# Latent attention on one Trainium2 core: a branch's sum is copied out of PSUM by ScalarE and divided in place by VectorE

## The chip, the cores and the metric

One Trainium2 chip, one of its cores. The metric is device microseconds of one execution of the whole program, as the median of several runs. Lower is better. The program is written in a tile framework whose scheduler runs a timeline model of its own while it builds, and writes down each engine's instructions in the order that this model gives. Every engine then works through its own list strictly in order.

## The reference, cut to what matters

Two layers over 512 latent tokens with a context of 256 tokens. Layer 0 has attention, layer 1 recurrences; each ends in a PEER expert network (16 experts out of 16384 for each of 8 heads). The change lies in the latent attention of layer 0:

```
p = softmax(concat(scores of latent keys, scores of context keys, sink))
out = sum(p_i @ v_i)                       # 4 blocks of 128 queries
branch A: all 512 latent keys + 256 context keys, no sink
branch B: keys within 128 positions + 256 context keys, with sink
y = concat(A, B) @ w_out;   h = h + gate * y
```

Each branch has 8 heads of width 64. The kernel multiplies the values with unnormalised exponentials and divides by their sums afterwards.

## The kernel before

Layer 0 runs in these stages: modulation and context attention; the projections of context and latents; the latent attention (`attention`, L488, the loop at L531); then `peer_lat` (L916), the expert network of the latents. The context's own expert network is done by gathering: `gather_run` (L714) fetches, for each of two context blocks, 128 times 128 rows of `peer_u` and then 128 times 128 rows of `peer_v` by indirect DMA. One gather means one indirect DMA that GpSimd (POOL) issues (L722, L731) and one VectorE instruction over 128x1024 that uses it up: a product with a sum (L724), or a scaled addition to `gacc` (L736, the first at L734). Five buffers named `grow` hold gathered rows. L726 is the Gelu between the two halves, L739 and L740 close a block. These gathers have the lowest priority (L887), so the scheduler strews them over VectorE's list between everything else: they run during the latent attention and far into `peer_lat`. The latent block 0 (`REST`) is gathered likewise after them.

For each of 4 query blocks `att_block` (L432) does two branches. For each branch `attend` (L387) runs four times: TensorE makes scores into two `pbig` tiles (L401, L404, masks L407), VectorE takes the negated maximum (L411, with the sink L413), ScalarE the exponentials (L417), TensorE transposes them (L424), ScalarE copies them out of PSUM (L425), and TensorE multiplies with the values (L429) into one quarter of the bank `pv`, role "o", tile `po`. There is a single bank of that role (L530). After the fourth call VectorE inverts the sums (L453) and spreads them (L456), TensorE turns them (L459), ScalarE copies that out (L462), and VectorE multiplies `po` with it into half of `mT` (L463). Only then may the next branch's L429 write `po`. `out_block` (L236) multiplies `mT` with the output weights (L800), VectorE applies the gate (L221), GpSimd adds (L222), and `norm` (L533) makes the block's input of the expert network: L99 scales, L107 transposes, L115 shifts; for blocks 1 to 3 L123 and L124 split the result into two parts, `xh` and `xl`. `mT` has one buffer.

`peer_lat` can't start its products (L806, from `project`, L932) before the last block's `xl`. It then computes scores, picks experts, and runs 128 chunks of `hidden` (L817): load `u` (`peer_uT`), split it (L793 on ScalarE, L794 on VectorE), multiply (L806, L808). `peer_values` (L824) does the second half with `v` (L841, weighting L854), and L869 and L870 add its result to the latents. Layer 1 begins with L99 on the sums.

Of the kernel before, what the change touches and what calls it, by code (L numbers as in the profile page):

```python
# [18 lines left out]
AF = mybir.ActivationFunctionType  # L19
OP = mybir.AluOpType  # L20
# [30 lines left out]
class Kern:  # L51
# [380 lines left out]
    def att_block(self, pool, out, qT, b, lat):  # L432

        nc = self.nc
        if not lat:
            mix = pool.tile([128, D], F32, name="mix")
            for branch in range(2):
                for i in (0, 2):
                    for r in range(2):
                        self.attend_ctx(pool, qT, b, branch, r, i, mix)  # L440
            return self.mix_T(out, [mix[:, k * 128:(k + 1) * 128] for k in range(KD)])
        mT = out.tile([128, KD, 128], F32, name="mT", bufs=1)
        for branch in range(2):
            pv = self.pm("o")
            nm, sm = (pool.tile([128, 8], F32, name=x, bufs=2) for x in ("nm", "sm"))
            for i in range(4):
                self.attend(pool, qT, b, branch, i, pv, nm, sm)
            if branch:
                es = pool.tile([128, 8], F32, name="es", bufs=2)
                nc.vector.tensor_tensor(es, nm, self.sink, op=OP.add)  # L450
                nc.scalar.activation(es, es, AF.Exp)
                nc.vector.tensor_tensor(sm, sm, es, op=OP.add)
            nc.vector.reciprocal(sm, sm)  # L453

            x = pool.tile([128, 8, 64], F32, name="rcp")
            nc.vector.tensor_copy(x, sm.unsqueeze(2).to_broadcast([128, 8, 64]))  # L456
            pr = self.pm("a")
            for i in range(4):
                nc.tensor.matmul(pr[:, i * 128:(i + 1) * 128], x[:, 2 * i:2 * i + 2].rearrange("p h d -> p (h d)"),  # L459
                                 self.ident, start=True, stop=True)  # L460
            y = x.rearrange("p h d -> p (h d)")
            nc.scalar.activation(y, pr, AF.Copy)  # L462
            nc.vector.tensor_tensor(mT[:, 4 * branch:4 * branch + 4].rearrange("p c q -> p (c q)"), pv, y, op=OP.mult)  # L463
        return mT

    def att_out_ctx(self, pool, mTs):
# [1234 lines left out]
```

## Time and profile before

| | us |
|---|---|
| three runs | 4375.18, 4366.16, 4362.2; median 4366.16 |
| the profiled execution, its own time | 4357.14 |
| its span in the trace | 4355.4 |
| busy in the span: PE, DVE, ACT, POOL | 3926.1, 3415.4, 1783.2, 1520.6 |
| mean granted TensorE clock | 0.937 of full speed |

PE is TensorE's matmuls, PEld its weight loads, DVE VectorE, ACT ScalarE, POOL GpSimd. The page's shares are means over stages of different kinds, so the stages are read one by one: from a table of windows, then by what each engine waited for in a stage, then instruction by instruction in order of time. A row of the waits names the waiting instruction and what ended its wait; in the timeline the bracket behind a row holds the idle time before it and its releaser. Gathers have their DMA's cost apart from their VectorE cost: POOL only issues it.

### The profile page before, as it was taken

What the parts mean: (1) busy time and instruction counts of PE and PEld (TensorE: products, weight loads), DVE (VectorE), ACT (ScalarE), POOL (GpSimd) and SP (SyncE); (2) the same over time, 40 slices, a digit from 0 to 9 for tenths busy, and PEclk for the clock granted to TensorE, in tenths of its full rate; (3) what the DMA queues carried; (4) which work ended last, traced back from release to release, by engine and by line L of the source; (5) the groups of instructions that cost most, each with busy time, mean ns of one, the idle gap of its engine ahead of it and who ended that gap; (6) DMA issues with size and microseconds to landing.
All of it is one profiled execution on the core that took longest, in us unless ns stands there. A gap on an engine that the chain in (4) does not pass through costs nothing.

```text
span 4355.4 us, 63744 instructions
## 1 busy us (share of the span) xinstructions
PE 3926.1 (90%) x22484; PEld 3452.8 (79%) x22484; DVE 3415.4 (78%) x7022; ACT 1783.2 (41%) x3482; POOL 1520.6 (35%) x1252
## 2 busy tenths in 40 slices
PE   7995588799799888999999699999988999899998
PEld 5684356599789887778888569988988899888887
DVE  2249988899998898898899766665998888777555
ACT  3310243332345674434333433334234577433433
POOL 0016666655434445443444101221333333322000
PEclk9997588799999998999999799999999999999999
DMA  7748877899878999999999411022688999999765
GB/s 309 262 161 288 272 261 264 300 322 334 290 262 295 344 346 362 338 342 337 347 343 342 138 57 38 31 88 69 223 284 290 306 343 342 368 338 330 238 220 162
DMA packets 439674, 1152.81 MB, mean 265 GB/s; under 512 B 39173, under 2 KB 209541, under 8 KB 428089
## 3 DMA queue, kind: packets, MB, share of 16 engines
q1 hardware_dynamic: 289592, 586.63, 38.8%
q0 software_dynamic: 147456, 536.94, 35.2%
q10 hardware_dynamic: 2304, 25.17, 1.6%
q8 instruction: 177, 2.90, 0.3%
q14 instruction: 145, 1.18, 0.1%
HBM read 1045.30 MB, written 103.28 MB: 264 GB/s over the span
## 4 chain that ended last, share of the span: by engine, by line
PE 61%; DVE 16%; DMA 11%; issue 6%; ACT 4%; POOL 2%; SPq 0%; DVEq 0%; ACTq 0%; POOLq 0%
PE acc L841 23%; PE ph L806 8%; PE pa L806 6%; DMA u<-peer_uT 4%; DVE grow L724 4%; PE ph L808 3%; PE pa L808 3%; DMA grow<-peer_u,gidx 3%; PE pa L288 3%; DMA grow<-peer_v,gidx 2%; DVE gacc L736 2%; PE pt L780 2%; DVE ul L794 2%; PE pa L800 2%; PE pa L162 1%
## 5 line engine op out<-in xcount | busy, mean ns | idle before, releaser
L731 POOL DMA_INDIRECT grow<-peer_v,gidx x512 | 692.8, 1353 | 878.6 <-DVE gacc L736 739.7
L722 POOL DMA_INDIRECT grow<-peer_u,gidx x512 | 665.8, 1300 | 744.1 <-DVE hid L724 437.8
L806 PE MATMUL ph<-xh,uh 128*128 128x384 f32 x2048 | 722.9, 353 | 104.3 <-ACT uh L793 78.1
L806 PE MATMUL ph<-xl,uh 128*128 128x384 f32 x2048 | 710.0, 347 | 0.3 <-DVE xl L124 0.3
L736 DVE SCALAR_TENSOR_TENSOR gacc<-grow,gw,gacc 128x1024 f32<-128x1024 f32 x508 | 655.6, 1291 | 33.7 <-DMA grow<-peer_v,gidx 31.1
L724 DVE CUSTOM_DVE_ANT_0 grow<-grow,gx 128x1024 f32<-128x1024 f32 x512 | 620.8, 1224 | 48.1 <-DMA grow<-peer_u,gidx 45.1
L793 ACT ACTIVATE uh<-u 128x1024 fp32r<-128x1024 f32 x340 | 358.2, 1057 | 521.0 <-DMA u<-peer_uT 218.5
L794 DVE TENSOR_TENSOR ul<-u,uh 128x1024 fp32r<-128x1024 f32 x340 | 415.7, 1225 | 127.8 <-ACT uh L793 104.2
L806 PEld LDWEIGHTS ph<-xh,uh 128*128 128x128 f32 x2048 | 402.1, 196 | 128.1 <-ACT uh L793 93.2
L841 PE MATMUL acc<-vl,wh 128*128 128x512 f32 x1536 | 480.2, 394 | 1.6 <-DVE vl L794 1.6
L841 PE MATMUL acc<-vh,wl 128*128 128x512 f32 x1536 | 475.6, 391 | 0.0
L841 PE MATMUL acc<-vh,wh 128*128 128x512 f32 x1536 | 409.4, 396 | 17.4 <-ACT vh L793 9.9
L808 PE MATMUL ph<-xh,ul 128*128 128x384 f32 x2048 | 410.8, 339 | 7.0 <-DVE ul L794 6.7
L806 PEld LDWEIGHTS ph<-xl,uh 128*128 128x128 f32 x2048 | 402.7, 197 | 2.8 <-DVE xl L124 0.8
L793 ACT ACTIVATE wh<-w 128x384 fp32r<-128x384 f32 x256 | 134.3, 525 | 636.3 <-PE acc L841 496.4
L808 PEld LDWEIGHTS ph<-xh,ul 128*128 128x128 f32 x2048 | 359.8, 189 | 11.0 <-DVE ul L794 8.9
L794 DVE TENSOR_TENSOR vl<-v,vh 128x1024 fp32r<-128x1024 f32 x256 | 312.7, 1221 | 51.8 <-ACT vh L793 50.4
L841 PEld LDWEIGHTS acc<-vh,wh 128*128 128x128 f32 x1536 | 285.6, 189 | 75.1 <-ACT vh L793 11.8
L841 PEld LDWEIGHTS acc<-vh,wl 128*128 128x128 f32 x1536 | 288.7, 188 | 62.4 <-issue 0.9
L841 PEld LDWEIGHTS acc<-vl,wh 128*128 128x128 f32 x1536 | 286.2, 189 | 61.4 <-DVE vl L794 4.1
L793 ACT ACTIVATE vh<-v 128x1024 fp32r<-128x1024 f32 x256 | 270.0, 1056 | 48.6 <-PE acc L841 37.1
L780 PE MATMUL pt<-oi,oj 128*128 128x128 f32 x1536 | 211.5, 287 | 35.9 <-DVE oj L769 14.8
(549 smaller groups left out, 6570.4 us busy)
## 6 DMA issues: line engine op xcount, KB each, us to landing
u<-peer_uT SPq DMA_DIRECT2D x256, 512.0 KB
v<-peer_v SPq DMA_DIRECT2D x256, 512.0 KB
w<-mod_w SPq DMA_DIRECT2D x48, 1024.0 KB
Gd<-stage SPq DMA_DIRECT2D x48, 1024.0 KB
Hd<-hw SPq DMA_DIRECT2D x240, 192.0 KB
w<-Hd SPq DMA_DIRECT2D x240, 192.0 KB
u<-rec_w SPq DMA_DIRECT2D x52, 512.0 KB
g<-Gd SPq DMA_DIRECT2D x16, 1536.0 KB
```

What stands on the lines that cost most here:

```text
L288: nc.tensor.matmul(ps[:, b * 128:(b + 1) * 128], aT[:, kd, b * 128:(b + 1) * 128], w[:, kd, :], start=kd == 0, stop=kd == KD - 1)
L722: nc.gpsimd.indirect_dma_start(out=u, out_offset=None, in_=A[f"peer_u{layer}"], in_offset=bass.IndirectOffsetOnAxis(ap=row(s), axis=0))
L724: nc.vector.tensor_tensor_reduce(u, u, x, 1.0, 0.0, OP.mult, OP.add, hid[:, s:s + 1])
L731: nc.gpsimd.indirect_dma_start(out=u, out_offset=None, in_=A[f"peer_v{layer}"], in_offset=bass.IndirectOffsetOnAxis(ap=row(s), axis=0))
L736: nc.vector.scalar_tensor_tensor(acc, u, w[:, s:s + 1], acc, op0=OP.mult, op1=OP.add)
L780: nc.tensor.matmul(ps[:, t * 128:(t + 1) * 128], oj[:, t], oi[:, t], start=True, stop=True)
L793: nc.scalar.activation(hi, x, AF.Copy)
L794: nc.vector.tensor_tensor(lo, x, hi.bitcast(F32), op=OP.subtract)
L800: self.nc.tensor.matmul(ps, w[:, kd, :], x[:, kd, :], start=kd == 0, stop=kd == KD - 1)
L806: self.nc.tensor.matmul(ps, wh[:, kd, :], b[:, kd, :], start=kd == 0 and b is xh, stop=False)
L808: self.nc.tensor.matmul(ps, wl[:, kd, :], xh[:, kd, :], start=False, stop=kd == KD - 1)
L841: nc.tensor.matmul(acc[b][f], a[:, b * 128:(b + 1) * 128], c[:, f * 512:(f + 1) * 512], start=k + t == 0, stop=k == len(chunks) - 1 and t ...
```

## The change

ScalarE copies the four finished products of a branch from `po` into the branch's half of `mT`, and VectorE's multiplication with the spread inverse reads and writes that half in place. The copy stands in the program ahead of the inversion of the sums. Two lines are added, so what follows carries line numbers two higher (L453 becomes L455, L456 L458, L459 L461, L462 L464, L463 L465, L724 L726, L726 L728, L727 L729, L734 L736, L736 L738, L739 L741, L740 L742, L869 L871, L870 L872); the copy is L454.

```diff
                 nc.vector.tensor_tensor(sm, sm, es, op=OP.add)
+            m = mT[:, 4 * branch:4 * branch + 4].rearrange("p c q -> p (c q)")
+            nc.scalar.activation(m, pv, AF.Copy)
             nc.vector.reciprocal(sm, sm)
...
             nc.scalar.activation(y, pr, AF.Copy)
-            nc.vector.tensor_tensor(mT[:, 4 * branch:4 * branch + 4].rearrange("p c q -> p (c q)"), pv, y, op=OP.mult)
+            nc.vector.tensor_tensor(m, m, y, op=OP.mult)
         return mT
```

The scheduler draws up all engines' lists anew. Three places follow.

First place: ScalarE, from the last exponentials of block 0's branch B (128x512) on; 128x768 are block 1's. Before:

```order
L417 ACTIVATE P,sm<-pbig,nm 128x512 x4
L451 ACTIVATE es<-es 128x8
L417 ACTIVATE P,sm<-pbig,nm 128x768
L425 ACTIVATE PT<-pt 128x512 x2
L462 ACTIVATE rcp<-pa 128x512
L425 ACTIVATE PT<-pt 128x512
```

And of the change:

```order
L417 ACTIVATE P,sm<-pbig,nm 128x512 x4
L451 ACTIVATE es<-es 128x8
L417 ACTIVATE P,sm<-pbig,nm 128x768
L454 ACTIVATE mT<-po 128x512
L425 ACTIVATE PT<-pt 128x512 x3
L417 ACTIVATE P,sm<-pbig,nm 128x768
L425 ACTIVATE PT<-pt 128x512
L417 ACTIVATE P,sm<-pbig,nm 128x768
L464 ACTIVATE rcp<-pa 128x512
L425 ACTIVATE PT<-pt 128x512
L454 ACTIVATE mT<-po 128x512
```

The copy of branch A stands behind the first exponentials of block 1, ahead of all that frees TensorE's transposes for branch B's last products.

Second place: VectorE, block 1, where the Gelu of the first gathered block (`gw`) is used. Before:

```order
L456 COPY rcp<-sm 128x512
L99 TENSOR_SCALAR xn<-h_100,nm_y 128x1024
L727 TENSOR_TENSOR gw<-gw,ggate 128x128
L413 TENSOR_TENSOR nm<-nm,msink 128x2
L734 TENSOR_SCALAR gacc<-grow,gw 128x1024
```

Of the change:

```order
L99 TENSOR_SCALAR xn<-h_100,nm_y 128x1024
L726 ISA grow,hid<-grow,gx 128x1024
L726 ISA hid 128x1
L413 TENSOR_TENSOR nm<-nm,msink 128x2
L729 TENSOR_TENSOR gw<-gw,ggate 128x128
L736 TENSOR_SCALAR gacc<-grow,gw 128x1024
```

The last gather of the first half (two rows: product and accumulator read) now stands behind L99. On ScalarE, at the same place, the Gelu moved behind the shifts of that L99. Before:

```order
L726 ACTIVATE gw<-hid 128x128
L425 ACTIVATE PT<-pt 128x512 x2
L417 ACT_TABLE_LOAD
L417 ACTIVATE P,sm<-pbig,nm 128x640 x2
L115 ACTIVATE x_4312<-pa,b_323,a_321 128x128 x4
```

Of the change:

```order
L425 ACTIVATE PT<-pt 128x512 x2
L454 ACTIVATE mT<-po 128x512
L115 ACTIVATE x_4312<-pa,b_323,a_321 128x128 x4
L728 ACT_TABLE_LOAD
L728 ACTIVATE gw<-hid 128x128
L417 ACT_TABLE_LOAD
L417 ACTIVATE P,sm<-pbig,nm 128x640 x2
```

Four shifts and a copy stand ahead of the Gelu that stood behind it before.

Third place: VectorE at the end of layer 0, where the latents' sums (L869, L870) meet the last gathers. Before:

```order
L736 SCALAR_TENSOR_TENSOR gacc<-grow,gw,gacc 128x1024
L870 TENSOR_TENSOR h_102<-h_102,v 128x1024
L869 TENSOR_TENSOR v<-acc_14640,v 128x512
L869 TENSOR_TENSOR v<-acc_14641,v 128x512
L736 SCALAR_TENSOR_TENSOR gacc<-grow,gw,gacc 128x1024
L870 TENSOR_TENSOR h_103<-h_103,v 128x1024
L736 SCALAR_TENSOR_TENSOR gacc<-grow,gw,gacc 128x1024 x2
L81 TENSOR_SCALAR nm_y<-nm_v 128x1
L739 TENSOR_TENSOR gacc<-gacc,grow 128x1024
L794 TENSOR_TENSOR wgl<-wg,wgh 128x128
L740 TENSOR_TENSOR h_100<-h_100,gacc 128x1024
L99 TENSOR_SCALAR xn<-h_101,nm_y 128x1024
```

Of the change:

```order
L871 TENSOR_TENSOR v<-acc_14647,v 128x512
L738 SCALAR_TENSOR_TENSOR gacc<-grow,gw,gacc 128x1024
L872 TENSOR_TENSOR h_101<-h_101,v 128x1024
L872 TENSOR_TENSOR h_102<-h_102,v 128x1024
L741 TENSOR_TENSOR gacc<-gacc,grow 128x1024
L871 TENSOR_TENSOR v<-acc_14648,v 128x512
L871 TENSOR_TENSOR v<-acc_14649,v 128x512
L742 TENSOR_TENSOR h_100<-h_100,gacc 128x1024
L872 TENSOR_TENSOR h_103<-h_103,v 128x1024
L81 TENSOR_SCALAR nm_y<-nm_v 128x1
L796 TENSOR_TENSOR wgl<-wg,wgh 128x128
L99 TENSOR_SCALAR xn<-h_101,nm_y 128x1024
```

Between the first of these sums and layer 1's first L99 there stood five gathers, and there stands one.

## Rows read from the trace of the kernel before

**Rows 1.** The page, part 1: busy us (share of the span), instructions.
```profile
PE 3926.1 (90%) x22484; PEld 3452.8 (79%) x22484; DVE 3415.4 (78%) x7022; ACT 1783.2 (41%) x3482; POOL 1520.6 (35%) x1252
```
**Rows 2.** Windows: stage, PE, PEld, DVE, ACT, POOL busy (instructions), granted clock, DMA share, GB/s.
```profile
460.00:556.50 96.50, 36.12 (x145) 22.81 (x143) 88.44 (x231) 13.59 (x33) 64.56 (x53) 0.57 0.80 272
556.50:853.00 296.50, 246.29 (x1413) 179.01 (x1413) 247.57 (x278) 117.07 (x268) 200.85 (x157) 0.82 0.80 270
853.00:1000.00 147.00, 145.61 (x924) 145.42 (x925) 146.27 (x458) 44.15 (x55) 85.00 (x61) 0.98 0.92 329
1000.00:1400.00 400.00, 355.27 (x2008) 346.68 (x2007) 366.49 (x982) 165.32 (x276) 159.81 (x117) 0.95 0.85 289
1400.00:1690.00 290.00, 241.42 (x1435) 233.01 (x1434) 259.84 (x314) 191.81 (x445) 149.13 (x104) 0.89 1.01 346
1690.00:2424.00 734.00, 712.80 (x3712) 606.90 (x3711) 649.27 (x993) 285.70 (x471) 317.26 (x264) 0.99 0.93 341
```
**Rows 3.** Timeline of TensorE around 557 us: start, us, instruction, count.
```profile
557.27 3.68 PE L429 MATMUL po<-PT,v 128*64 128x128 f32 x32 [29.68 <-DVE mT L463]
```
**Rows 4.** VectorE's waits from 556.5 to 853 us: total, times, longest.
```profile
DVE gacc L736 <- DMA grow<-peer_v,gidx: 16.6, 18, 1.8
DVE nm L411 <- PE pbig L407: 15.3, 10, 3.4
DVE nm L411 <- PE pbig L404: 6.8, 3, 4.4
```
**Rows 5.** Timeline of VectorE, after the first L463 and at the stage's end.
```profile
556.53 0.69 DVE L463 TENSOR_TENSOR mT<-po,rcp 128x512 f32<-128x512 f32 x1
...
569.53 0.96 DVE L411 TENSOR_REDUCE nm<-pbig 128x1 f32<-128x768 f32 x1 [4.44 <-PE pbig L404]
...
573.40 0.96 DVE L411 TENSOR_REDUCE nm<-pbig 128x1 f32<-128x768 f32 x1 [2.09 <-PE pbig L404]
...
579.17 0.69 DVE L221 TENSOR_TENSOR ot<-pa,gate 128x512 f32<-128x512 f32 x1 [2.53 <-PE pa L800]
...
852.93 1.22 DVE L124 TENSOR_TENSOR xl<-xt,xh 128x1024 fp32r<-128x1024 f32 x1
...
854.67 1.22 DVE L740 TENSOR_TENSOR hc<-hc,gacc 128x1024 f32<-128x1024 f32 x1
```
**Rows 6.** Groups by line and form, 460 to 860 us: busy, mean ns | idle before.
```profile
L736 DVE SCALAR_TENSOR_TENSOR gacc<-grow,gw,gacc 128x1024 f32<-128x1024 f32 x127 | 167.7, 1320 | 18.3 <-DMA grow<-peer_v,gidx 16.6
L463 DVE TENSOR_TENSOR mT<-po,rcp 128x512 f32<-128x512 f32 x8 | 5.5, 687 | 0.1
L462 ACT ACTIVATE rcp<-pa 128x512 f32<-128x512 f32 x8 | 4.8, 596 | 10.0 <-PE pa L459 10.0
L115 ACT ACTIVATE x<-pa,b,a 128x128 f32<-128x128 f32 x8 | 3.0, 460 | 1.5 <-PE pa L107 1.5
```
**Rows 7.** Instructions of L319, VectorE, both inputs in SBUF: ns min/median/max.
```profile
L319 DVE TENSOR_TENSOR qk<-qk,qt x10: 674/682/853, 224.6 to 394.8; 128x512 f32<-128x512 f32 x10
```
**Rows 8.** Instructions of L731, POOL's issue of a gather: ns min/median/max.
```profile
L731 POOL DMA_INDIRECT grow<-peer_v,gidx x512: 932/1141/4622, 597.8 to 4011.6; - x171
```
**Rows 9.** Timeline of ScalarE around 604 us, the Gelu of the first gathered block.
```profile
603.58 1.28 ACT L726 ACT_TABLE_LOAD   x1
604.88 0.31 ACT L726 ACTIVATE gw<-hid 128x128 f32<-128x128 f32 x1
```
**Rows 10.** The page, part 3: the queue of the 1024 gathers: packets, MB, share.
```profile
q0 software_dynamic: 147456, 536.94, 35.2%
```
**Rows 11.** TensorE's and ScalarE's longest waits from 1000 to 1690 us.
```profile
PE ph L806 <- ACT uh L793: 47.6, 23, 5.9
...
ACT uh L793 <- DMA u<-peer_uT: 112.1, 39, 8.6
```
**Rows 12.** TensorE's wait from 2400 to 2450 us, and VectorE's L99 that ends it.
```profile
PE pa L107 <- DVE xn L99: 16.7, 1, 16.7
...
2442.13 0.75 DVE L99 TENSOR_SCALAR xn<-h,nm_y 128x1024 f32<-128x1024 f32 x1 [2.13 <-ACT nm_y L85]
```

## The prediction

> **What bounds the kernel now.** I read the page first, then windows, then who waited for whom, then single instructions, and the order of the lists beside them. The page alone misleads: TensorE is busy 90% of the span, VectorE 78% [rows 1], which says that ScalarE has room and TensorE none. The windows show that this isn't so where the change lies [rows 2]. In the latent attention, 460 to 853 us, TensorE is busy 36 of 96 and 246 of 296 us, at a granted clock of 0.57 and 0.82, while VectorE is busy 88 of 96 and 248 of 296 us: this stage is VectorE's. Its list mixes the attention's small steps with the gathers of the context, and it stops for whichever isn't ready. After 853 us TensorE is busy 145.6 of 147 us, so a later start of the expert network is a later end of that piece. From 1000 to 1690 us none is full, but the DMA engines are (share 1.01 from 1400 on), and TensorE waits 47.6 us for ScalarE's split of `u`, which itself waits 112.1 us for the load of `u` [rows 11]. From 1690 to 2424 us TensorE bounds again, 713 of 734 us [rows 2].
>
> **The wait that the change aims at.** TensorE waited 29.68 us, once, for the first L463 [rows 3]. This is the only large one; the other seven L463 held nobody up for long. It is TensorE's idle time in a stage that VectorE bounds, so most of it was free. What counts is what VectorE lost because the products came late: after that L463 it waited 4.44 and 2.09 us for scores of block 1 and 2.53 us for the gate's input [rows 5].
>
> **The change, part by part.**
>
> *The copy.* Eight copies 128x512 from PSUM on ScalarE. The same shape at L462 takes 0.596 us [rows 6], so 4.8 us in all, in a stage where ScalarE is busy 131 of 393 us [rows 2]. In its list the first copy stands behind block 1's first exponentials and ahead of what waits for it on TensorE, which came to that point at about 527 us in the old run (557.27 - 29.68 [rows 3]). I put 0 on the path; if each copy met its block's end, 4.8.
>
> *The multiplication.* It reads `mT` in place of PSUM. PSUM and SBUF took 0.687 us [rows 6]; two SBUF inputs of that size took 0.682 us at L319 [rows 7]. Difference 0. POOL's issue of a gather takes 0.93 us at least and 1.14 us as median [rows 8]: something already stretches many. [...]
>
> *The wait that goes.* With the bank freed by about 527 us, branch B's 32 products [rows 3] move into TensorE's idle time, and the scores of block 1 are ready when VectorE asks. So 4.44 + 2.09 = 6.5 us go. The 2.53 us for the gate stay, because those products still follow the second division. Bounds: 0 and -9.1.
>
> *What is late next: the lists.* This is the larger part, and the diff doesn't show it. Counted on VectorE's list, 148 gathers stand between the first L463 and the last `xl` (L124) before, 158 after the change; `hc` (L740), which stood behind that `xl`, now stands ahead of it. So ten gathers and one addition move ahead of the point for which the expert network waits. A gather costs VectorE 1.32 us [rows 6], the addition 1.2 [rows 5]: 10 x 1.32 + 1.2 = 14.4 us. Some of this falls into waits that VectorE has anyway: 15.3 us, ten times, for masked scores [rows 4]. I take a third, 5.1, because the new gathers stand mostly in branch B's stretches and the waits in branch A's: +9.3 us. Bounds: all the waits filled, 14.4 - 15.3 = -0.9; or each gather at the stage's pace, (852.93 - 556.53)/148 = 2.00 us [rows 5], for the gathers wait for their own DMA too (16.6 us [rows 4]): 21.2.
>
> *A wait that is added.* The Gelu of the gathered block used to run ahead of block 0's shifts; now it stands behind four shifts that follow L99 by way of TensorE. Four times 0.460 [rows 6], a table load of 1.28 and the Gelu's 0.31 [rows 9] make 3.4 us after L99 ends, beside TensorE's transposes; VectorE has one gather (about 1.2) and a step of 0.15 us ahead of `gw`. All else on VectorE is queued behind it, gathers and maxima alike. At least 2 us, I take +3, at most 5; 0 if the gathers catch up afterwards.
>
> *What is given back.* From that `xl` to the first weighting of `peer_values` (L854) 276 gathers stand before, 266 after. One moves 536.94 MB / 1024 = 0.524 MB [rows 10], at the 346 GB/s of the stretch where the DMA engines are full [rows 2] 1.5 us. Ten are 15 us if the DMA engines bound all of it, 0 if TensorE does. The lead shrinks from ten to one between chunk 37 and chunk 133 of the splits, where TensorE is idle for want of `u` [rows 11]: I take -9. Bounds 0 and -15.
>
> *The end of layer 0.* TensorE waited 16.7 us there for L99, VectorE's first step of layer 1 [rows 12]. Five gathers stood between the sums of the first latent block and that L99, one stands now: 4 x 1.32 = 5.3 us, of which I take -4, because L99 also waited 2.13 us for ScalarE [rows 12]. Bounds 0 and -5.3.
>
> After that the lists of all engines become the same again within layer 1, and I expect a constant shift.
>
> **Sum.** -6.5 + 9.3 + 3 - 9 - 4 = -7.2 us, against the profiled execution's own 4357.1: 4349.9. That execution lies 9.0 us under the median of the runs shown, 4366.2, so on the median 4359.0. About 0.3%, 13 us, is what a measurement of this kernel can tell from no change: the forecast is no change that can be told, leaning to faster.
>
> **The rivals.**
>
> *The gathers cost more than the wait was worth* (slower). Place: between the first division and the last `xl`. For it: VectorE is nearly full in that stage, and its gathers wait for DMA eighteen times [rows 4], so a gather more may cost the pace of 2.00 us. Then -6.5 + 21.2 + 3 = +17.7 with nothing given back, since TensorE bounds from 853 us on [rows 2]: 4384. It decides from 1.53 us per moved gather: (13 + 6.5 - 3 - 1.2)/10. Against it: the waits for masked scores, and the DMA-bound stretch later.
>
> *All waits collapse* (faster). TensorE runs ahead from 527 us on, every wait of VectorE for scores is filled by the moved gathers, and the later stretch is the DMA engines' alone: -9.1 - 0.9 + 0 - 15.2 - 5.3 = -30.5: 4336. For it: the DMA share of 1.01 and 112.1 us of waiting for `u` [rows 2, 11]. Against it: VectorE must still issue each maximum in its place in the list.
>
> *The change doesn't do what it says.* The products of branch B wait for ScalarE's copies from `pt`, as they did for L463, so that the 6.5 us come back at another name: 9.3 + 3 - 9 - 4 = -0.7, 4365.5. Against it: ScalarE is idle two thirds of the stage [rows 2].
>
> **How the numbers follow.** The forecast's case gets 0.62, with an own range of 4345 to 4373; three tenths of it lie more than 13 us below the median. The slower rival gets 0.14, the faster 0.17, the one without effect 0.07. Faster: 0.17 + 0.19 = 0.36. Same: 0.43 + 0.07 = 0.50. Slower: 0.14. The range reaches to both outer rivals, 4336 to 4384, and leaves out what lies beyond either, some 2 in 10.
>
> **What would show it.** Right: no wait of TensorE for `mT`; no wait of VectorE for the scores behind the first division; a new one of 2 to 5 us at `gw`; the last `xl` at 853 + 5.8, about 859 us, later although a wait went; the first L841 at the old place or a few us earlier; layer 1's first L99 some 7 us earlier than 2442 us, and the same shift at the end. Wrong: a last `xl` before 845 us (the waits were worth more than the ten gathers) or after 865 us; a different shift at 1690 us than at the end of layer 0; or a shift that still changes in layer 1. A wait of VectorE or ScalarE for the copy itself would upset the first step.

## The result, and the profile after

The changed kernel took 4402.83 us (median of four runs, 4395.22 to 4409.2), the kernel before 4367.02 us beside it: 35.8 us more, ratio 1.0072, 95% interval 1.0057 to 1.0087. The forecast was 4359.0 us with a range of 4336 to 4384. The execution in the trace is the slowest of the four (4409.2, span 4407.4), the one of before lies 9.9 us under its median; so their spans differ by 52.0 us, of which 16 are chance of the two executions.

The page, part 1, of the changed kernel (busy us, share, instructions), against [rows 1]:

```profile
PE 3959.2 (90%) x22484; PEld 3471.4 (79%) x22484; DVE 3419.7 (78%) x7022; ACT 1789.8 (41%) x3490; POOL 1533.9 (35%) x1252
```

Eight instructions more on ScalarE and the same shares: the page tells nothing. The windows, columns as in [rows 2]:

```profile
460.00:556.50 96.50, 41.48 (x188) 27.81 (x188) 88.21 (x228) 15.61 (x37) 63.97 (x54) 0.58 0.80 271
556.50:853.00 296.50, 249.02 (x1298) 172.24 (x1295) 232.27 (x261) 109.81 (x249) 190.26 (x145) 0.77 0.74 247
853.00:1000.00 147.00, 120.99 (x723) 116.59 (x723) 135.71 (x360) 41.78 (x64) 81.94 (x64) 0.89 0.89 315
```

The latent attention is where it goes wrong. From 556.5 to 853 us VectorE, which sets the pace there, was busy 247.6 us before [rows 2] and is busy 232.3 now. TensorE does 1298 matmuls in that window where it did 1413, and 723 in place of 924 in the next one. Its granted clock in these two windows is 0.77 and 0.89 where it was 0.82 and 0.98.

The first copy and what follows it, on ScalarE's timeline, and the instruction of VectorE that released the copy:

```profile
551.15 0.60 ACT L454 ACTIVATE mT<-po 128x512 f32<-128x512 f32 x1 [24.91 <-DVE ge L645]
553.83 1.09 ACT L425 ACTIVATE PT<-pt 128x512 f32<-128x512 f32 x2 [2.07 <-PE po L429]
```
```profile
550.43 0.69 DVE L645 TENSOR_TENSOR ge<-tpf,marks 128x512 bf16<-128x512 bf16 x1
```

`ge` is a tile of the context's routing (L645, on VectorE). The copy needs nothing from it but its memory: `mT` lies in a pool that takes over memory which the routing gives up at about 551 us (e4 and e16 below bear this out). TensorE's longest waits from 460 to 700 us (total, times, longest):

```profile
PE pt L424 <- ACT P L417: 26.7, 6, 8.8
PE po L429 <- ACT mT L454: 22.6, 1, 22.6
```

So the wait of [rows 3] is still there, 22.6 us for 29.7, under another name. It isn't where the time is lost. ScalarE stood idle at this place before too, and longer, because its next work needs TensorE's products; here it is on before's timeline, with the second division of block 0 on VectorE's, before and after:

```profile
559.29 1.08 ACT L425 ACTIVATE PT<-pt 128x512 f32<-128x512 f32 x2 [34.68 <-PE po L429]
```
```profile
570.62 0.69 DVE L463 TENSOR_TENSOR mT<-po,rcp 128x512 f32<-128x512 f32 x1
```
```profile
571.62 0.69 DVE L465 TENSOR_TENSOR mT<-mT,rcp 128x512 f32<-128x512 f32 x1 [1.57 <-ACT mT L454]
```

With the copy ScalarE goes on at 553.83 us where it went on at 559.29, and block 0's second division is 1.0 us late (in e1, the same kernel again, 1.9 us early). The loss comes in the blocks behind it. VectorE's waits from its first division, 560.2 us, to 893 us, against [rows 4]:

```profile
DVE nm L411 <- PE pbig L407: 20.3, 11, 3.2
DVE gacc L738 <- DMA grow<-peer_v,gidx: 18.5, 26, 3.4
DVE nm L411 <- PE pbig L404: 11.0, 5, 3.8
DVE gw L729 <- ACT gw L728: 6.2, 1, 6.2
DVE ot L221 <- PE pa L802: 5.8, 1, 5.8
DVE grow L726 <- DMA grow<-peer_u,gidx: 5.2, 7, 1.1
DVE mT L465 <- ACT rcp L464: 1.6, 1, 1.6
DVE mT L465 <- ACT mT L454: 1.6, 1, 1.6
```

The waits for scores grew from 22.1 to 31.3 us (28.6 in e1) where I expected them to shrink. On VectorE's timeline the stage ends, against [rows 5], 45.9 us later (34.5 in e1):

```profile
878.63 1.22 DVE L742 TENSOR_TENSOR hc<-hc,gacc 128x1024 f32<-128x1024 f32 x1
...
898.83 1.22 DVE L124 TENSOR_TENSOR xl<-xt,xh 128x1024 fp32r<-128x1024 f32 x1
```

The parts themselves cost what was said (groups by line and form, busy, mean ns | idle before), against [rows 6]:

```profile
L465 DVE TENSOR_TENSOR mT<-mT,rcp 128x512 f32<-128x512 f32 x8 | 5.5, 686 | 3.2 <-ACT rcp L464 1.6 <-ACT mT L454 1.6
L464 ACT ACTIVATE rcp<-pa 128x512 f32<-128x512 f32 x8 | 4.8, 599 | 16.0 <-PE pa L461 16.0
L454 ACT ACTIVATE mT<-po 128x512 f32<-128x512 f32 x8 | 4.8, 598 | 33.4 <-DVE ge L645 24.9 <-PE po L429 8.5
```

### The profile page after: what moved, and what is told of

It reads as the page before. It is cut to its first block, busy times and chain, and to the rows that moved or that the text cites. A ratio compares the mean times of both kernels' runs of the same rounds, so it can differ in the third digit from the quotient of the medians.

```text
span 4407.4 us, 63765 instructions
## 1 busy us (share of the span) xinstructions
PE 3959.2 (90%) x22484; PEld 3471.4 (79%) x22484; DVE 3419.7 (78%) x7022; ACT 1789.8 (41%) x3490; POOL 1533.9 (35%) x1252
## 4 chain that ended last, share of the span: by engine, by line
PE 60%; DVE 15%; DMA 12%; issue 6%; ACT 4%; POOL 2%; SPq 0%; DVEq 0%; ACTq 0%; POOLq 0%
PE acc L843 23%; PE ph L808 8%; PE pa L808 6%; DMA u<-peer_uT 4%; DVE grow L726 4%; DMA grow<-peer_u,gidx 3%; PE ph L810 3%; PE pa L810 3%; PE pa L288 2%; PE pa L802 2%; PE pt L782 2%; DVE ul L796 2%; DMA grow<-peer_v,gidx 2%; POOL grow L724 2%; DVE gacc L738 1%
## 5 line engine op out<-in xcount | busy, mean ns | idle before, releaser
L733 POOL DMA_INDIRECT grow<-peer_v,gidx x512 | 710.2, 1387 | 894.3 <-DVE gacc L738 717.1
L724 POOL DMA_INDIRECT grow<-peer_u,gidx x512 | 666.2, 1301 | 749.3 <-DVE hid L726 443.3
L738 DVE SCALAR_TENSOR_TENSOR gacc<-grow,gw,gacc 128x1024 f32<-128x1024 f32 x508 | 657.2, 1294 | 40.4 <-DMA grow<-peer_v,gidx 37.2
L726 DVE CUSTOM_DVE_ANT_0 grow<-grow,gx 128x1024 f32<-128x1024 f32 x512 | 622.4, 1228 | 54.0 <-DMA grow<-peer_u,gidx 53.7
```

The source lines that it names most:

```text
L724: nc.gpsimd.indirect_dma_start(out=u, out_offset=None, in_=A[f"peer_u{layer}"], in_offset=bass.IndirectOffsetOnAxis(ap=row(s), axis=0))
L726: nc.vector.tensor_tensor_reduce(u, u, x, 1.0, 0.0, OP.mult, OP.add, hid[:, s:s + 1])
L733: nc.gpsimd.indirect_dma_start(out=u, out_offset=None, in_=A[f"peer_v{layer}"], in_offset=bass.IndirectOffsetOnAxis(ap=row(s), axis=0))
L738: nc.vector.scalar_tensor_tensor(acc, u, w[:, s:s + 1], acc, op0=OP.mult, op1=OP.add)
```

## The experiments

All 17 runs in one table, each beside the kernel before on its chip. "Gathers" stand on VectorE's list ahead of the last `xl` of the latent attention. "Idle" is the sum of the gaps in VectorE's timeline from 460 us to that `xl`; "layer 1" the start of the last `aTl` (L124), with which layer 1 sets off; "last stage" the time from the first to the last product with the gate in the second expert network (L854 of before). These four columns are of one execution, the difference is of medians.

| run | gathers | idle | last xl | layer 1 | last stage | median less before's | ratio, 95% interval |
|---|---|---|---|---|---|---|---|
| before | 256 | 55.4 | 852.9 | 2468.5 | 553.9 | | |
| changed kernel | 267 | 81.1 | 898.8 | 2512.0 | 554.7 | +35.8 | 1.0057 to 1.0087 |
| e1 the same again | 267 | 75.7 | 887.5 | 2495.6 | 555.4 | +40.3 | 1.0064 to 1.0111 |
| e2 copies of branch 1 only | 264 | 65.1 | 876.5 | 2499.8 | 573.1 | +34.3 | 1.0058 to 1.0100 |
| e3 changed, mT in lat_h | 242 | 52.8 | 829.5 | 2447.1 | 569.7 | -28.8 | 0.9904 to 0.9948 |
| e4 before, mT in lat_h | 254 | 58.8 | 853.4 | 2473.2 | 554.1 | -15.1 | 0.9953 to 0.9987 |
| e5 changed, gathers held | 256 | 94.5 | 893.2 | 2521.5 | 577.6 | +48.2 | 1.0083 to 1.0131 |
| e6 before, 12 gathers ahead | 268 | 63.9 | 876.5 | 2492.6 | 553.9 | +10.6 | 1.0011 to 1.0036 |
| e7 first copy only | 256 | 60.1 | 856.4 | 2485.1 | 572.1 | +27.6 | 1.0043 to 1.0082 |
| e8 the other seven | 253 | 55.6 | 851.5 | 2467.5 | 569.9 | +1.9 | 0.9998 to 1.0025 |
| e9 a small read in their place | 266 | 56.1 | 866.5 | 2474.1 | 560.0 | +4.5 | 1.0005 to 1.0043 |
| e10 copies on VectorE | 253 | 44.7 | 845.0 | 2468.6 | 555.3 | +0.1 | 0.9988 to 1.0015 |
| e11 branch 0's copies, mT in lat_h | 242 | 70.2 | 850.8 | 2475.5 | 555.4 | -1.1 | 0.9985 to 1.0025 |
| e12 VectorE's copies, mT in lat_h | 237 | 51.2 | 833.4 | 2467.5 | 554.9 | +2.6 | 0.9982 to 1.0015 |
| e13 the wait alone | 256 | 51.9 | 850.5 | 2460.9 | 554.5 | -5.0 | 0.9980 to 1.0015 |
| e14 dead copies | 267 | 74.3 | 888.8 | 2499.8 | 582.2 | +46.5 | 1.0084 to 1.0138 |
| e15 copies of branch 0 only | 263 | 62.2 | 868.3 | 2481.1 | 554.5 | +16.7 | 1.0030 to 1.0062 |
| e16 e3 again | 242 | 50.3 | 829.2 | 2443.5 | 569.4 | -30.0 | 0.9931 to 0.9967 |
| e17 e4 again | 254 | 55.6 | 853.7 | 2481.0 | 554.5 | -8.8 | 0.9969 to 0.9996 |

The ratios come from runs side by side on one chip and differ from the medians' difference by up to 8 us. One execution isn't a mean: the changed kernel itself reached its last `xl` at 898.8 and at 887.5 us. Nor can a stage of one trace be taken off a median: e8's last stage is 16 us longer than before's, and its median lies only 1.9 us over before's. The expectations of e3, e4, e8 and e10 to e12 count gathers ahead of the last `xl` wrongly (those that fall short of the first block's end were halved); the table has them right. For e3 "7 gathers fewer" ought to read 14, 18 us. `lat_o` and `lat_h` are the two pools of the latent attention; `mT` is taken from `lat_o` (`out` in the code), and in the runs marked so from `lat_h` (`pool`).

I began with three theories. **M**: the loss is ScalarE standing 25 us behind its first copy (**M+**: with all that this sets off). **O**: it is the gathers that come ahead, and longer waits. **S**: it is the copies' own time ahead of the exponentials.

**e1 and e2.** e1 is the changed kernel. e2, against before:

```diff
+            m = mT[:, 4 * branch:4 * branch + 4].rearrange("p c q -> p (c q)")
+            if branch:
+                nc.scalar.activation(m, pv, AF.Copy)
...
-            nc.vector.tensor_tensor(mT[:, 4 * branch:4 * branch + 4].rearrange("p c q -> p (c q)"), pv, y, op=OP.mult)
+            nc.vector.tensor_tensor(m, m if branch else pv, y, op=OP.mult)
```

> The changed kernel once more, as the control of these runs. All theories: 4395 to 4410 us, 28 to 43 us over the kernel before; last xl at 895 to 902; the first copy waits some 25 us on ScalarE for VectorE's ge.

> Only branch 1's result is copied (4 copies instead of 8); branch 0's division reads its bank and writes mT as before. 264 gathers stand ahead of the last xl (before 256, changed kernel 267). Theory M (the loss is ScalarE standing 25 us behind the first copy, which waits for mT's memory): no copy comes before the memory is free, so no such wait, and 4362 to 4372 us. Theory O (the loss is the new order: gathers and longer waits ahead of the last xl): 8 gathers x 1.32 us = 10.6 us and about as much in waits again, 4385 to 4395 us, last xl at 870 to 885. Theory S (ScalarE's own time in copies, ahead of exponentials): half the loss, 4380 to 4390 us.

e2 has no copy that waits for `mT`'s memory, and still lost 34.3 us, nearly as much as e1. M alone doesn't hold. But in the trace 19 us of it are in the last stage (573.1 for 553.9), some 2900 us after the attention.

**e3 and e4.** `mT` from `lat_h`, where it doesn't take over the routing's memory; e3 on the changed kernel, e4 on the kernel before:

```diff
-        mT = out.tile([128, KD, 128], F32, name="mT", bufs=1)
+        mT = pool.tile([128, KD, 128], F32, name="mT", bufs=1)
```

> The changed kernel with mT taken from pool lat_h instead of lat_o, so that it lies elsewhere in memory. The first division stands behind 64 gathers instead of 109, 249 gathers ahead of the last xl. Theory M: the first copy waits under 3 us on ScalarE, the loss goes, 4355 to 4370 us. Theory O: 7 gathers fewer than before, 9 us less, 4350 to 4362 us, last xl at 840 to 848. Theory S: eight copies as before, the loss stays, 4395 to 4410 us.

> The kernel before (no copy, division from the bank) with mT taken from pool lat_h. 255 gathers ahead of the last xl. Theory M, on what held the bank in the kernel before: the first division no longer waits for the routing's end and PE's wait of 29.7 us for it shrinks under 10 us without any copy; the time 4360 to 4370 us as VectorE sets the pace. Rival (VectorE is late because routing is ahead of the division on its list whatever the memory): the wait stays at 25 to 30 us. Theory O: 4363 to 4369 us, last xl at 848 to 856.

e4 answers what the 29.7 us of [rows 3] were. Its first division, on VectorE's timeline, and what is left of TensorE's wait for it between 460 and 700 us:

```profile
476.12 0.69 DVE L463 TENSOR_TENSOR mT<-po,rcp 128x512 f32<-128x512 f32 x1
```
```profile
PE po L429 <- DVE mT L463: 1.6, 1, 1.6
```

The division comes 80.4 us earlier [rows 5] without any copy. So VectorE wasn't late to read a finished bank: the division could not write, and the scheduler had put it behind the routing for that reason. With the memory free the eight copies do no harm: e3 lies 13.7 us under e4. S falls.

**e5 and e6**, on the gathers. e5 holds the second context block's gathers of the changed kernel behind the last `xl`; e6 pulls some of them ahead in the kernel before (e5 against the changed kernel, e6 against before):

```diff
+        if after is not None:
+            nc.vector.tensor_copy(hid, after.bitcast(F32))
...
+                with tc.high_priority(offset=-2 * BACK):
+                    self.gather_run(0, self.second, self.hc[1], 1, self.xs[1][:, 0, 256:384])
```
```diff
+                    if b == NL - 1:
+                        late = self.gather_run(0, self.second, self.hc[1], 1, 2)
+                        hid = next(late)
+                        self.nc.vector.scalar_tensor_tensor(self.h[b][:, :1], hid[:, 1:2], 0.0, self.h[b][:, :1], op0=OP.mult, op1=OP.add)
```

> The changed kernel, with the second context block's gathers held behind the last xl by a data dependency (its hid tile is first filled from that xl); all else stands in the same order, 256 gathers ahead of the last xl. Theory O (gathers ahead of the last xl delay it and the delay stays to the end): 11 x 1.32 us + 1.2 us for the block's end, some 16 us earlier at the last xl than the changed kernel (870 to 880) and 14 to 18 us faster in all, 10 to 25 us over before. Theory M+ (ScalarE's stand behind the first copy and what it sets off is all of it): same as the changed kernel within 5 us, and the time saved ahead comes back as waits. Rival G (gathers put off are given back in the stage after): last xl earlier, the end the same, 35 to 40 us over before.

> The kernel before, without any copy, in which 12 gathers of the second context block are made to come ahead of the last block's norm (one small operation that leaves h as it is waits for the second of them). Theory O: 12 x 1.32 + 1.2 = 17 us later at the last xl (868 to 875), 15 to 20 us slower than before in all. Theory M+ or rival G: last xl later but the end within 5 us of before.

e6: 12 gathers ahead of the last `xl` cost 0.23%, 10 us, and not the 17 that their VectorE time comes to. e5 gave nothing back, and not at its last `xl` either: with 11 gathers fewer ahead that `xl` came at 893.2 us, between the changed kernel's 887.5 and 898.8, and VectorE stood 13 to 19 us longer instead. What these gathers cost among the changed kernel's other lists stays open, the more so as e5's last stage took 577.6 us, 23 more than the changed kernel's.

**e7 and e8**, the copies apart (e7 against before):

```diff
+            first = b == 0 and branch == 0
+            if first:
+                nc.scalar.activation(m, pv, AF.Copy)
...
+            nc.vector.tensor_tensor(m, m if first else pv, y, op=OP.mult)
```

(e8 has `if not first` and the two sources exchanged.)

> Only the first of the eight copies (block 0, branch 0), the one that waits for mT's memory; the other seven divisions read their banks. 256 gathers ahead of the last xl as before. Theory M+: ScalarE stands some 25 us and all of the loss is there, 30 to 40 us over before. Theory O: the stand costs only what e1 lost over e2, 5 to 12 us over before, last xl at 858 to 866.

> The other seven copies, the first division reading its bank; 254 to 255 gathers ahead of the last xl. Theory M+: no copy before the memory is free, within 5 us of before. Theory O: the order ahead of the last xl is that of before, so no loss either, -5 to +5 us, last xl at 848 to 858. Theory S (copies ahead of exponentials in ScalarE's queue): seven eighths of the loss, 28 to 36 us over before.

These speak for the first copy: alone 27.6 us, the others 1.9. But each runs in lists of its own, neither in those of the changed kernel, and e7's last `xl` is only 3.5 us late and its last stage 18 us longer; here are that stage's first and last products, of before and of e7, from VectorE's timelines:

```profile
3764.03 0.56 DVE L854 TENSOR_TENSOR w<-w,g 128x384 f32<-128x384 f32 x1 [2.64 <-DMA w<-Hd]
...
4317.89 0.56 DVE L854 TENSOR_TENSOR w<-w,g 128x384 f32<-128x384 f32 x1 [0.91 <-DMA w<-Hd]
```
```profile
3781.59 0.56 DVE L858 TENSOR_TENSOR w<-w,g 128x384 f32<-128x384 f32 x1 [2.36 <-DMA w<-Hd]
...
4353.74 0.56 DVE L858 TENSOR_TENSOR w<-w,g 128x384 f32<-128x384 f32 x1 [0.75 <-DMA w<-Hd]
```

553.9 against 572.1 us, in a stage that no edit touches: the scheduler drew its lists otherwise. So the 27.6 us can't be put down to the wait alone.

**e9 to e12.** Theory **P**: the number of gathers that the scheduler weaves into the attention sets the time. **W**: the added work is paid where it is done. e9 puts a read of 8 columns in the copy's place, with the division of before; e10 puts the copies on VectorE (both against the changed kernel); e11 and e12 have `mT` in `lat_h` (e11 against before):

```diff
-            nc.scalar.activation(m, pv, AF.Copy)
+            nc.scalar.activation(pool.tile([128, 8], F32, name="nn", bufs=1), pv[:, :8], AF.Copy)
...
-            nc.vector.tensor_tensor(m, m, y, op=OP.mult)
+            nc.vector.tensor_tensor(m, pv, y, op=OP.mult)
```
```diff
-            nc.scalar.activation(m, pv, AF.Copy)
+            nc.vector.tensor_copy(m, pv)
```
```diff
+            if not branch:
+                nc.scalar.activation(m, pv, AF.Copy)
...
+            nc.vector.tensor_tensor(m, pv if branch else m, y, op=OP.mult)
```

(The last is e11's; e12 is e10 with `mT` in lat_h.)

> The kernel before with a read of 8 columns of the bank by ScalarE, into a scratch tile, where the changed kernel has its copy; the division reads the bank and writes mT as before. No copy, no earlier release of the bank, no wait for mT's memory on ScalarE; but the order that the scheduler makes of it is close to the changed kernel's: 10 gathers more ahead of the last division, 10 ahead of the last xl. Theory P (the order in which the scheduler interleaves the attention with the gathers is the loss, whatever the added instruction does): the last division after 825 us, the last xl at 870 to 895, 20 to 40 us over before. Theory M+ or any theory that needs the copy's work, the bank or the wait: within 6 us of before.

> The changed kernel with the eight copies on VectorE (8 x 0.65 us more there). Its order has 254 to 255 gathers ahead of the last xl, 5 fewer ahead of the last division than before, and the last expert stage in the order of before. Theory P: last division at 805 to 813, last xl at 846 to 855, -15 to +3 us to before. Theory W (the added work itself is paid on the engine that does it): 5 us or more over before.

> mT in lat_h, and only branch 0's result copied on ScalarE (4 copies). 249 gathers ahead of the last xl, 15 fewer than before ahead of the last division; the last expert stage is in the order of before, not in that of e3, whose stage took 570 us from the first to the last gate product where before takes 554. Theory P: last xl at 828 to 840 as in e3 and 554 us in that stage, 4322 to 4340 us, 30 to 45 us under before. If the order of the last stage is of no account: 4340 to 4350 us.

> mT in lat_h and the eight copies on VectorE. 246 to 247 gathers ahead of the last xl, 22 fewer than before ahead of the last division; last expert stage in the order of before. Theory P: last division at 770 to 785, last xl at 820 to 832, 4315 to 4335 us, 35 to 50 us under before. Theory W: 5 us over e11.

P falls three times. e9 has one gather fewer ahead than the changed kernel, about as much idle time on VectorE as before, and costs 0.24%, like e6 with 0.23%: ten to twelve gathers ahead are worth some 10 us (intervals 2 to 19 and 5 to 16). e11 and e12 have 14 and 19 gathers fewer than before and gain nothing. In e11 VectorE stands 14.8 us longer than before, and the last `xl` comes hardly earlier. e12's timeline of VectorE at the end of layer 0 shows why:

```profile
2416.68 0.75 DVE L99 TENSOR_SCALAR xn<-h,nm_y 128x1024 f32<-128x1024 f32 x1
...
2452.34 1.23 DVE L742 TENSOR_TENSOR h<-h,gacc 128x1024 f32<-128x1024 f32 x1
...
2461.72 0.75 DVE L99 TENSOR_SCALAR xn<-h,nm_y 128x1024 f32<-128x1024 f32 x1 [0.41 <-ACT nm_y L85]
```

Its expert network is done 25.5 us earlier than before [rows 12], but the last L99 needs the latent block that is gathered, and that one closes at 2452.3 us: the gathers that were put off come due there. Layer 0 has two ends, TensorE's and that of VectorE's gathers, and layer 1 waits for the later one. e10 speaks against W: copies, in-place division and the early release of the bank, without a wait on ScalarE, cost nothing that can be told (interval -5 to +7 us, and W asked for 5 or more). The 0.65 us a copy that were expected of VectorE were my estimate: its copies of that size out of PSUM took 0.69 us in before (L1240).

**e13 to e15** are on the wait. M now says that the wait itself costs; **Q** that it is made good, and that the lists cost which the scheduler drew on account of it. e13 (against before), e14 (against the changed kernel: its copies, but the bank is divided) and e15 (against before):

```diff
+            if b == 0 and branch == 0:
+                nc.scalar.activation(m[:, :8], nm, AF.Copy)
...
+            nc.vector.tensor_tensor(m, pv, y, op=OP.mult)
```
```diff
-            nc.vector.tensor_tensor(m, m, y, op=OP.mult)
+            nc.vector.tensor_tensor(m, pv, y, op=OP.mult)
```
```diff
+            if not branch:
+                nc.scalar.activation(m, pv, AF.Copy)
...
+            nc.vector.tensor_tensor(m, pv if branch else m, y, op=OP.mult)
```

> The kernel before with one added instruction: ScalarE writes 8 columns of mT in block 0, branch 0, at the place of the changed kernel's first copy, so that it waits there for mT's memory (VectorE's ge) with all that is behind it; every engine's list is otherwise that of before, the last expert stage too. Theory M (the wait itself costs): 15 to 30 us over before, VectorE standing 15 us or more longer ahead of the last xl. Theory Q (the wait is made good within block 1, and only the order that the scheduler made on account of it costs): within 6 us of before, last xl at 850 to 862.

> The eight copies as in the changed kernel, but the division reads the bank again and overwrites them. 267 gathers ahead of the last xl, one fewer than in the changed kernel ahead of the last division; the last expert stage in another order than before (15 to 20 us more there, as in e2, e3, e5, e7, e8). Theory M and theory Q alike: the loss of the changed kernel and that of the stage, 40 to 60 us over before. If the in-place division or the bank given up early costs: under 25 us.

> Only branch 0's result is copied (4 copies, the first with its wait), mT in lat_o; 263 gathers ahead of the last xl, 5 more than before ahead of the last division, the last expert stage in the order of before. Theory M: the wait's price as in e13 and half of the order's, 20 to 35 us over before. Theory Q: 8 to 20 us over before.

e13 has every list of before, one instruction apart, and its wait is the changed kernel's (ScalarE's waits, 460 to 620 us, then TensorE's to 700):

```profile
ACT mT L455 <- DVE ge L646: 25.1, 1, 25.1
```
```profile
PE po L429 <- DVE mT L466: 29.5, 1, 29.5
```

It costs nothing that can be told: -5.0 us, interval 0.9980 to 1.0015 (-9 to +7 us), VectorE idle 51.9 us. In the lists of before ScalarE stood idle at this place anyway, for 34.68 us. M falls. e14 has the copies for nothing, and the bank is held till the division as before; its two waits are nearly e13's, and yet its last `xl` (888.8) and layer 1's start (2499.8) come as late as e1's; it loses 46.5 us, and its last stage is 28 longer:

```profile
ACT mT L454 <- DVE ge L645: 24.7, 1, 24.7
```
```profile
PE po L429 <- DVE mT L465: 31.1, 1, 31.1
```

So neither the bank given up nor the division in place is the loss. e15 decides nothing between M and Q: 16.7 us by the medians and 20 by the ratio, where Q ends and M begins at 20.

**e16 and e17** repeat e3 and e4 side by side.

> e3 once more. If the copies gain where mT's memory is free: 4335 to 4350 us, 20 to 35 us under before, last xl at 825 to 835. If e3 was a chance of that chip: within 10 us of before.

> e4 once more, beside e16: 4355 to 4365 us, 5 to 15 us under before, and 10 to 20 us over e16.

The gain stands: 0.51%, and 21.2 us between the two. On ScalarE's timeline of e16 the first two copies now wait for TensorE's products alone:

```profile
470.26 0.60 ACT L454 ACTIVATE mT<-po 128x512 f32<-128x512 f32 x1 [2.12 <-PE po L429]
...
525.94 0.60 ACT L454 ACTIVATE mT<-po 128x512 f32<-128x512 f32 x1 [0.42 <-PE po L429]
```

**Where the lists lose it.** VectorE's waits of more than 0.15 us from one block's second division to the next one's, added up:

| | before | changed | e1 | e8 | e13 |
|---|---|---|---|---|---|
| to block 1's | 12.5 | 27.0 | 22.9 | 12.9 | 11.2 |
| to block 2's | 12.3 | 12.4 | 8.3 | 9.8 | 11.5 |
| to block 3's | 10.3 | 17.0 | 21.7 | 11.7 | 8.4 |
| to the last `xl` | 6.1 | 10.0 | 8.4 | 6.3 | 7.7 |

From block 0's second division up to block 1's every kernel whose lists were drawn with the waiting copy in them (the changed kernel, e1, e5, e7, e14, e15) stands 17.1 to 27.0 us; every other one with `mT` in its old place (before, e2, e6, e8, e9, e10, and e13, which has the wait in before's lists) stands 9.9 to 12.9. That fits Q: not the wait, but the lists that the scheduler drew on account of it. In the blocks where the waits grew TensorE's granted clock fell as well; here is block 1 of before and of the changed kernel, columns as in [rows 2]:

```profile
570.60:645.30 74.70, 66.76 (x416) 47.74 (x416) 61.85 (x83) 35.65 (x80) 50.28 (x38) 0.89 0.72 242
```
```profile
571.60:670.00 98.40, 85.24 (x433) 57.51 (x431) 70.84 (x90) 38.09 (x84) 59.97 (x44) 0.79 0.64 214
```

Such a figure is a mean: in the changed kernel's block 1 the granted clock was 1.00 from 573 to 603 us and 0.50 from 604 to 613 (L429: 281 and 433 ns a matmul). To block 1's division it is 0.79 (e1 0.80) for 0.89, to block 3's 0.70 (e1 0.71) for 0.78, but to block 2's 0.83 (e1 0.88) for 0.82. Whether TensorE's slower products (L429 in block 1: 302 ns a matmul before, 337 in the changed kernel) are a part of the cause of VectorE's waits or only follow from its own waits, no run here separates.

Two places can be seen. In block 1 the Gelu stands behind four shifts of block 0's norm, as foreseen; ScalarE's timeline of the changed kernel, against [rows 9]:

```profile
615.46 1.50 ACT L115 ACTIVATE x<-pa,b,a 128x128 f32<-128x128 f32 x4
616.99 1.28 ACT L728 ACT_TABLE_LOAD   x1
618.28 0.31 ACT L728 ACTIVATE gw<-hid 128x128 f32<-128x128 f32 x1
```

VectorE waits 6.2 us for it, of the 14.5 that it stands longer up to block 1's division (3.0 of 10.4 in e1). In block 3 the maximum of finished scores stands on VectorE's list behind four gathers and the product with the gate; TensorE's and VectorE's timelines of e1, then VectorE's of before at the same place:

```profile
767.06 0.70 PE L404 MATMUL pbig<-kTc,qT 64*128 64x256 f32 x4
...
778.53 1.54 PE L424 MATMUL pt<-cm,P 128*128 128x128 f32 x6 [9.74 <-ACT P L417]
```
```profile
774.23 1.82 DVE L411 TENSOR_REDUCE nm<-pbig 128x1 f32<-128x768 f32 x2
```
```profile
761.00 0.94 DVE L411 TENSOR_REDUCE nm<-pbig 128x1 f32<-128x768 f32 x1
```

In e1 the scores are done at 767.8 us and their maximum starts 6.5 us later; the exponential needs the maximum, TensorE's transposes wait 9.74 us for the exponential, the next scores are behind them, and VectorE waits for those. In the changed kernel's own trace the same stretch is 8.3 us and TensorE's wait 9.3; before, three gathers stood there, the stretch was 4.9 us, and TensorE's wait for the exponential 4.5.

## Why the prediction was wrong

A sum that comes near it: 11 gathers ahead cost about 10 us (e6, e9), and VectorE stands 25.7 us longer (changed) or 20.3 (e1) ahead of the last `xl`; 30 to 36 together, measured 35.8 and 40.3. It joins waits of single executions with a cost taken from medians, so how close it comes is partly luck. That the standing comes from the order of the lists is argued by elimination: the wait (e13), seven copies (e8), the copying and the early release (e10), the use of the copies (e14) are each taken away or tried alone, and only e13 does so in lists that stay as they are. The changed kernel's lists without copies, and its copies in the lists of before, were not tried. Which change of order makes the waits is seen in two places and not proved by undoing them.

Two steps failed, the wait that goes and, with the larger error, the lists. Step by step:

- *The copy, 0*: its time (0.598 us) and that of the in-place multiplication (0.686) were right, and the copies as such cost nothing that can be told (e8, e10). What was missed is what the copy has to wait for. I asked when its input is ready and not when its output's memory is.
- *POOL's issues of gathers*, no term of the sum: they stayed as they were. The changed kernel's first in-place multiplication (560.23 us, 0.69 us long) lies wholly inside an issue of a gather (560.15 us, 0.97 us long, where the shortest of before is 0.93 [rows 8]): the two ran side by side. The issues of `peer_v` rows from 460 to 860 us took 1.27 us on the mean before, 1.28 in e13, which divides out of PSUM, and 1.28 in the changed kernel, 1.31 in e1. What makes many of them longer than 0.93 us, before as after, no run separates.
- *The wait that goes, -6.5*: **this step failed.** "With the bank freed by about 527 us" was wrong; it was freed at 551.75, and the waits for scores grew by 9.2 us (6.5 in e1) in place of shrinking.
- *The lists, +9.3*: **this step failed too.** The count of gathers was right (148, then 158), and about 10 us is what they cost. But I took the number of gathers for all that a new order does. The waits that I wanted to fill with them grew: VectorE stands 20 to 26 us longer, and of that only the 3 us at `gw` were in the sum.
- *The wait at `gw`, +3*: 6.2 and 3.0 us in two executions; right in kind and about in size.
- *Given back, -9*: from +45.9 us at the last `xl` to +38.8 at the first weighting (1692.58 and 1731.43 us), and +34.5 to +23.3 in e1: 7 and 11, right in size. The reason that I gave, the DMA time of the gathers put ahead, isn't borne out: e2, with 8 gathers ahead, gave nothing back there, and e3 and e16, with 14 fewer, gained another 11 and 13 us.
- *The end of layer 0, -4*: from that weighting to layer 1's start it came out at +4.7. The five gathers were one, as said, but the stretch from the first of the latents' sums to layer 1's first L99 shrank by only 0.9 us (17.9 to 17.0); the rest came ahead of it.
- Afterwards I expected a constant shift. In layer 1 it grew by 8.5 us, from +43.5 at its start (+46.9 at its last `xl`) to +52.0 at the end, and by 6.9 in e1.

Of the rivals the slower one was right in its place, with 17.7 us where 35.8 came, but not in its reason: VectorE's waits for the gathers' own DMA hardly grew (16.6 to 18.5 us). That the change doesn't do what it says was true in a way that I hadn't thought of: TensorE's wait stayed because memory, not the bank, was its cause. Of the warning signs named at the end three appeared: a last `xl` after 865 us, a shift that still changes in layer 1, and a wait of ScalarE for the copy itself; that wait alone was harmless.

## What to carry to other kernels

When an instruction moves to another engine, look at when the memory of its *output* comes free, and which list will stand waiting for it: a name in the releaser's place that has nothing to do with the data was here the sign of reused memory (`ge` before `mT`, 24.91 us; 2.12 us for the products alone with `mT` in `lat_h`, e16), and a buffer placed elsewhere may be worth more than the edit. Under a scheduler that orders all lists anew, test an edit against one that leaves the lists alone (e13) and one that does the work for nothing (e14); without them e7 would have been taken for proof that the wait costs. And before a wait is called a loss, look whether the engine stood idle at that place before. Here the copy pays only with `mT` in `lat_h`: the two together took 0.51 and 0.74% off, 22 to 32 us, where the move of `mT` alone took 0.18 and 0.30%. Since e11 and e12, close relatives, gain nothing, that is the gain of this pairing with its lists, and no price of the copy.

## What was not expected

- A wait of 25.1 us at the head of ScalarE's list, in the middle of the attention, cost nothing that can be told (e13); VectorE, which sets the pace there, stood idle no longer than before (51.9 us for 55.4).
- An edit in layer 0 moved the last expert stage of layer 1 between two levels, 553.9 to 555.4 us in eleven of the traces and 569.4 to 582.2 in seven (e9 560.0). Kernels with the same lists kept to the same level (the changed kernel and e1, e3 and e16, e4 and e17). How much of it reaches the total is open: e8 and e16 have the long stage too.
- Executions of one and the same kernel lay up to 41 us apart (e11, 4347.02 to 4388.48), so that one trace doesn't settle a question of 10 us.
